# Starts of TensorE's tiles in SBUF: multiples of 128 bytes in the FFNs of a two-layer trunk

## The chip, the cores and the metric

The kernel runs on one core of a Trainium2 chip. The metric is the device time of one execution in microseconds (us), as the median of several runs. TensorE multiplies, VectorE (DVE), ScalarE (ACT) and GpSimd (POOL) do the elementwise work, and SyncE (SP) issues every DMA.

## The reference

A trunk of two layers over 512 positions of 1024 channels, in float32. Each layer is an FFN, a token mixer and a second FFN; layer 0 mixes by causal pooling over windows of 2 to 16 positions, layer 1 by forgetting attention with 16 heads. Each sub-layer first normalises and modulates x by the conditioning vector c:

```python
for i in range(DEPTH):
    mod = (silu(c) @ ada_w[i] + ada_b[i]).reshape(b_, 3, 3, D_MODEL)
    h = adaln(x, norm_g[i, 0], mod[:, 0, 0], mod[:, 0, 1])
    x = x + 0.5 * (1.0 + mod[:, 0, 2]) * swiglu(h, ffn_w_in[i, 0], ffn_w_out[i, 0])
    h = adaln(x, norm_g[i, 1], mod[:, 1, 0], mod[:, 1, 1])
    x = x + (1.0 + mod[:, 1, 2]) * mixer[i](h)
    h = adaln(x, norm_g[i, 2], mod[:, 2, 0], mod[:, 2, 1])
    x = x + 0.5 * (1.0 + mod[:, 2, 2]) * swiglu(h, ffn_w_in[i, 1], ffn_w_out[i, 1])

def swiglu(h, w_in, w_out):          # w_in (1024, 5632), w_out (2816, 1024)
    g, u = jnp.split(h @ w_in, 2, axis=-1)
    return (jax.nn.silu(g) * u) @ w_out
```

## The kernel before

**Layout.** Channels lie on the 128 partitions, positions along them: x is eight tiles of 128 x 512. The four FFNs have the numbers 0, 2, 3 and 5 of the six sub-layers (1 is the pooling, 4 the attention).

**Exact products in three.** A float32 operand is held as two float32r parts, hi and lo: ScalarE copies (and so rounds) the first, VectorE subtracts it from the source for the second (`split`, lines 144 to 150). `mm3` (lines 159 to 162) makes one product out of three matmuls: hi by hi, hi by lo, lo by hi. In the FFNs the held operand (TensorE's weight load, 128 x 128) is a block of the weights, wh or wl, and the streamed one is 512 or 256 columns of the activations: hhi and hlo, the normalised input, in the product "up" (`up`, lines 295 to 305), and gh and gl, the gated values, in the product "down" (lines 344 to 349 and `closing`, line 342).

**Loops.** An FFN goes in three chunks of 8, 8 and 6 of its 22 blocks of hidden channels. Up makes, for each block, two products (gate and value) over 8 tiles of channels: 2 x 8 x 3 = 48 matmuls. `gated` (line 286) makes gh and gl from them. Down takes, for each of the 8 tiles of output channels, the blocks of the chunk: 8 x 8 x 3 = 192 matmuls for a chunk of eight. Most are 512 wide; 256 wide are the first units and the last chunk of the FFNs that stand next to a norm, where the positions are done half by half.

**Weights.** SP loads a unit of weights into `raw` (line 153), in order of need, one DMA a unit; `split` writes wh and wl into the next of the slots (`slot`, line 64). Two slots are in the pool `wts` on the left side; a third, in the pool `more` on the right side, exists in FFNs 0, 2 and 3. The attention uses the same `weights` for its projections; there the held operand is a block of hhi or hlo and the streamed one 256 columns of the weights.

**Order.** SP's queue is in the order of the code in the FFNs; the first stage (before line 767) has SP, VectorE and ScalarE in order too. The other engines' order comes from the framework's list scheduling.

**Where the tiles begin.** The allocator places a tile on a multiple of 32 bytes within the partition, one after the other as the pools and sizes have it. For this program the starts, modulo 128 and modulo 512, are:

| tiles | modulo 128 | modulo 512 |
|---|---|---|
| hhi, hlo (streamed in up) | 32 | 416 |
| gh, gl (streamed in down) | 32 | 288 |
| wh, wl, raw in `wts` | 32 | 288 |
| wh, wl in `more` (third slot) | 96 | 480 |
| attention's q and k, groups 0 and 2 | 64 | 320 |
| attention's q and k, groups 1 and 3 | 32 | 288 |

The steps inside these tiles are 512, 1024 or 2048 bytes, so every slice begins at the same remainder of 128.

**Modulation.** `ada_open` (line 102) makes the small tiles of one sub-layer's modulation (`mods`) when the first work on them is due; they lie in the pool `pers` behind hlo.

Of the kernel before, what the change touches and what calls it, by code (L numbers as in the profile page):

```python
# [33 lines left out]
LAG = 3  # L34
SPAN = 16
EARLY = 4
WHOLE = ((0, S),)
# [4 lines left out]
def trunk(  # L42
# [21 lines left out]
    def slot(shape):  # L64
        """Both parts of a unit of weights, in the next of the slots."""
        pool = slots["pools"][slots["at"] % len(slots["pools"])]
        slots["at"] += 1
        return (pool.tile(shape, F32R, tag="wh", name="wh"), pool.tile(shape, F32R, tag="wl", name="wl"))

    dram = ctx.enter_context(tc.tile_pool(name="dram", bufs=1, space=DRAM))  # L70

    # ---- constants, parameters that stay on chip
    cond = right.tile([P, D], F32, name="cond")
    cst = pers.tile([P, 2, P], F32, name="cst")
    ident = cst[:, 0, :]
    ng = pers.tile([P, DEPTH * 3, KT], F32, name="ng")
    ab = pers.tile([P, DEPTH * 3, 3 * KT], F32, name="ab")
    x = pers.tile([P, KT, S], F32, name="x")
    ones = pers.tile([P, P], F32, name="ones")
    dve.memset(ones, 1.0)  # L80
    mhalf = pers.tile([P, GH], F32, name="mhalf")
    gp.memset(mhalf, -0.5)
    # the one table with all that an FFN takes, before anything waits for it
    act.activation(cond[:, 0:1], mhalf[:, 0:1], AF.Silu)

    # ---- modulation: column (dt, scale|shift) and gates of one sub-layer
    mods = {}

# [5 lines left out]
    def ada_work(i, u, raw):  # L94
        for r in range(2):
# [4 lines left out]
            )  # L100

    def ada_open(i):
        mods[i] = {
            "raw": pers.tile([P, 3 * KT], F32, name=f"mraw{i}"),
            "a": pers.tile([P, KT], F32, name=f"ma{i}"),
            "s": pers.tile([P, KT], F32, name=f"ms{i}"),
            "g": pers.tile([P, KT], F32, name=f"mg{i}"),
        }

# [18 lines left out]
    def ada_jobs(i, with_affine=True):  # L128
        """Pairs of a load and the work on it, for the steps of an FFN."""

        def work(u, raw):
            if u == 0:
                ada_open(i)
            ada_work(i, u, raw)
            if u == KT - 1:
                ada_affine(i, 0, KT)
            if u == KT + 3:
                ada_gate(i, i % 3 != 1)

        return [(lambda pool, u=u: ada_load(i, u, pool), lambda raw, u=u: work(u, raw))  # L140
                for u in range(0 if with_affine else KT, KT + 4)]

    # ---- exact splits of float32 into two float32r parts
    def split(parts, src, pieces=1):
# [7 lines left out]
    def weights(src, shape, pieces=4):  # L152
        raw = wts.tile(shape, F32, tag="raw", name="raw")
        nc.sync.dma_start(raw, src)
        parts = slot(shape)
        split(parts, raw, pieces)
        return parts
# [5 lines left out]

    # ---- pre-norm with adaLN
    hhi = pers.tile([P, KT, S], F32R, name="hhi")
    hlo = pers.tile([P, KT, S], F32R, name="hlo")

# [9 lines left out]
    def sumsq_pe(st, dt, t0, tn):  # L177
        """As sumsq, summed over the partitions too."""
        sq = tmp.tile([P, tn], F32, tag="sq", name="sq")
        act.activation(sq, x[:, dt, t0:t0 + tn], AF.Square)  # L180
        pe.matmul(st[:, :tn], ones, sq, start=dt == 0, stop=dt == KT - 1)  # L181

    def rsig(acc, t0, tn, summed=False):
        """1 / rms of each position, on every partition."""
        b0, bn = t0 // P, tn // P
        v = tmp.tile([P, NTB], F32, tag="v", name="v")
        if summed:
            st = acc
            for b in range(bn):
                bs = slice(b * P, (b + 1) * P)  # L190
                dve.tensor_tensor_reduce(out=st[:, bs], in0=st[:, bs], in1=ident, scale=1.0, scalar=0.0,
                                         op0=ALU.mult, op1=ALU.add, accum_out=v[:, b:b + 1])
            st = v
        else:
            st = bank("s")
            for b in range(bn):
                pe.matmul(st[:, b:b + 1], acc[:, (b0 + b) * P:(b0 + b + 1) * P], ones[:, 0:1],
                          start=True, stop=True)
        dve.tensor_scalar(out=v[:, :bn], in0=st[:, :bn], scalar1=1.0 / D, scalar2=EPS,
                          op0=ALU.mult, op1=ALU.add)  # L200
        gp.tensor_tensor(out=v[:, :bn], in0=v[:, :bn], in1=mhalf[:, :bn], op=ALU.pow)
        dg = tmp.tile([P, bn, P], F32, tag="dg", name="dg", bufs=1)
        dve.tensor_tensor(
            out=dg, in0=ident.unsqueeze(1).to_broadcast([P, bn, P]),
            in1=v[:, :bn].unsqueeze(2).to_broadcast([P, bn, P]), op=ALU.mult)
        r = bank("s")
        pe.matmul(r[:, :bn * P], ones, dg.rearrange("p b t -> p (b t)"), start=True, stop=True)
        return r
# [25 lines left out]

    # ---- half-step SwiGLU
    class Feed:
        """The weights of an FFN, unit by unit, in the order that the products take them."""

# [19 lines left out]
    def ffn(i, feed, jobs, then, begin=None, ahead_by=2, started=None):  # L258
# [3 lines left out]
        def job(pool, behind):  # L262
            """The work of the last load, behind what its engine does in this step; the next load."""
            if loaded:
                work, raw = loaded.pop()
                with tc.issue_after(behind):
                    work(raw)
                if ahead_by == 1:
                    return
            if jobs:  # L270
                load, work = jobs.pop(0)
                loaded.append((work, load(pool)))

        acc = new_acc() if then else None
        with (
# [6 lines left out]
            def g_tile():  # L282
                return (fp.tile([P, S], F32R, tag="gh", name="gh", bufs=JC + 1),
                        fp.tile([P, S], F32R, tag="gl", name="gl", bufs=JC + 1))

# [62 lines left out]
    def closing(wt, n, g, i, acc, then):  # L348
        """The last n tiles of a contraction: x is complete half by half of the positions."""
        for t0, tn in HALVES if then else WHOLE:  # L350
# [10 lines left out]

    # ---- multi-scale causal pooling
    class Pooling:
# [10 lines left out]
        def means(self, r, t0, tn):  # L374
            """Window means less the position itself."""
            m = mods[self.i]
# [39 lines left out]
        def mix(self, made, t0, tn):  # L416
            """The product by group, into x; returns the sums of squares."""
            sums = bank()
# [7 lines left out]

    # ---- forgetting attention
    def fox_first(pool):
        """Weights of the first q and k, ahead of time, in buffers that later hold v, q and k."""
        first = {}  # L430
# [18 lines left out]
    def fox(i, early_pool, first, second_half, then):  # L449
        acc2 = new_acc()  # L450
        with tc.tile_pool(name="fox", bufs=1, reuse_waits="tile") as fp:
            gains = fp.tile([P, 2], F32, name="gains")
            nc.sync.dma_start(gains, fox_gain)
            # the scores are held negated: their minimum is the bias of the exponential
            dve.tensor_scalar(out=gains[:, 0:1], in0=gains[:, 0:1], scalar1=-(HD ** -0.5),
# [5 lines left out]
            def forget():  # L461
                """cumsum(log_sigmoid(f)) by head, to DRAM to be spread over partitions."""
                bf = fp.tile([HEADS, 1], F32, name="bf")
# [17 lines left out]
                dve.scalar_tensor_tensor(out=e, in0=z, scalar=-1.0, in1=z, op0=ALU.mult, op1=ALU.min)  # L481
                # log1p(e) = log(w) + (e - (w - 1)) with w = 1 + e as rounded
                act.activation(e, e, AF.Exp)
# [12 lines left out]
            def projections(grp):  # L496
                """Steps that leave q, k by channel and v by position, split, for one group of heads."""
                made = {}
# [67 lines left out]
            class Head:  # L566
                """One head: scores and softmax by block of queries, then the product with v."""

# [88 lines left out]
            def early(ots):  # L657
                """The output projection of the first EARLY pairs of heads, into x."""
                held = {}
# [32 lines left out]

    # ---- the trunk
    ada_open(0)
    with tc.tile_pool(name="more", bufs=1, side="right", reuse_waits="tile") as more:
# [3 lines left out]
        with tc.tile_pool(name="start", bufs=2, reuse_waits="tile") as sp, in_order, ExitStack() as early:  # L699
            adas0 = early.enter_context(tc.tile_pool(name="adas", bufs=5, reuse_waits="tile"))  # L700
            w4 = early.enter_context(tc.tile_pool(name="w4", bufs=1, reuse_waits="tile"))
            # x by rows: 1 / rms is a scalar of each partition; then the channels to the partitions
            rows = sp.tile([P, NTB, D], F32, name="rows", bufs=1)
# [19 lines left out]
            def some_weights(kt, first=0, last=4):  # L723
                """The columns kt and kt + 1 of the units first .. last."""
                sl = slice(kt, kt + 2)
                if first == 0:
                    pieces[kt] = wts.tile([P, 4, 2, 2, P], F32, tag="raw", name="raw")
                for j in range(first, last):
# [166 lines left out]
```

## Time and profile before

| | us |
|---|---|
| median of 3 runs | 1861.64 |
| lowest and highest | 1855.61, 1865.67 |
| span of the profiled execution, first to last instruction | 1863.7 |
| TensorE busy in it | 1830.7 |
| VectorE, ScalarE, GpSimd busy in it | 985.8, 622.8, 107.0 |

The profile shows one execution; its own time stands in it as the span alone. A matmul's row has its start and a modelled end; since matmuls overlap, the time that one takes is read from its start to the next one's start. "x12" is a count of instructions, "<-" in a tile's name stands between what is written and what is read, and "<-" behind an idle time names what ended it.

### The profile page before, as it was taken

The numbers are of one execution on the slowest core, as the hardware profiler recorded it, in microseconds if no ns is written. First come the engines' busy times: TensorE is split into PE (matmuls) and PEld (weight loads), VectorE is DVE, ScalarE is ACT, GpSimd is POOL, SyncE is SP. The second block draws the span as 40 slices with busy tenths as digits, with TensorE's granted clock in tenths as the row PEclk, the third lists the DMA queues.
The fourth block names the chain that finished last, engine by engine and source line by source line (L and its number), as shares of the span: only waits on it lengthen the run. The fifth ranks groups of instructions, "written<-read, shape, count | busy, mean of one in ns | idle before, by whom it ended". The sixth has DMA issues, their size and how long they took to land.

```text
span 1863.7 us, 23985 instructions
## 1 busy us (share of the span) xinstructions
PE 1830.7 (98%) x9564; PEld 1549.0 (83%) x9564; DVE 985.8 (53%) x1947; ACT 622.8 (33%) x1242; POOL 107.0 (6%) x118
## 2 busy tenths in 40 slices
PE   6999999989999999999999999999999999999999
PEld 5888888879888888998888889988997888888887
DVE  7467466386466473363544534666666553432433
ACT  6323223244213232342222333354444442222221
POOL 0000000040000000110000001321010200000000
PEclk9999999989999999999999999999999899999999
DMA  9456465211266452231543531012111021321421
GB/s 365 181 203 262 178 228 225 92 68 70 112 257 240 169 212 93 73 136 70 199 173 120 190 126 69 25 69 86 63 63 63 30 107 57 124 96 63 135 91 68
DMA packets 45712, 244.66 MB, mean 131 GB/s; under 512 B 5392, under 2 KB 9872, under 8 KB 21792
## 3 DMA queue, kind: packets, MB, share of 16 engines
q1 hardware_dynamic: 45600, 243.13, 35.5%
q8 instruction: 75, 1.23, 0.3%
q14 instruction: 37, 0.30, 0.1%
HBM read 240.98 MB, written 2.13 MB: 130 GB/s over the span
## 4 chain that ended last, share of the span: by engine, by line
PE 96%; DVE 2%; ACT 1%; DMA 0%; issue 0%; SPq 0%; ACTq 0%; DVEq 0%
PE mm L160 29%; PE mm L161 28%; PE mm L162 28%; PE s L160 3%; PE s L161 3%; PE s L162 3%; PE mm L600 1%; PE mm L583 1%; PE mm L422 1%; DVE wl L149 1%; DMA cond<-c_in 0%; DVE x L225 0%; PE mm L181 0%; PE s L543 0%; DVE win L396 0%; DVE ada L97 0%
## 5 line engine op out<-in xcount | busy, mean ns | idle before, releaser
L161 PE MATMUL mm<-hlo,wh 128*128 128x512 f32 (+1 forms) x1512 | 566.8, 376 | 2.6 <-DVE hlo L764 2.6
L162 PE MATMUL mm<-hhi,wl 128*128 128x512 f32 (+1 forms) x1512 | 565.1, 376 | 0.5 <-DVE wl L149 0.5
L160 PE MATMUL mm<-hhi,wh 128*128 128x512 f32 (+1 forms) x1512 | 562.4, 377 | 1.7 <-ACT hhi L755 1.4
L148 ACT ACTIVATE wh<-raw 128x256 fp32r<-128x256 f32 (+2 forms) x528 | 311.4, 654 | 573.5 <-PE mm L161 325.6
L149 DVE TENSOR_TENSOR wl<-raw,wh 128x256 fp32r<-128x256 f32 (+2 forms) x528 | 359.8, 733 | 49.5 <-ACT wh L148 46.0
L161 PEld LDWEIGHTS mm<-hlo,wh 128*128 128x128 f32 x1512 | 283.9, 188 | 59.5 <-DVE hlo L764 3.1
L160 PEld LDWEIGHTS mm<-hhi,wh 128*128 128x128 f32 x1512 | 283.2, 188 | 59.3 <-ACT hhi L755 1.8
L162 PEld LDWEIGHTS mm<-hhi,wl 128*128 128x128 f32 x1512 | 284.0, 188 | 57.2 <-DVE wl L149 0.7
L290 DVE TENSOR_TENSOR sil<-sil,mm 128x512 f32<-128x512 f32 (+1 forms) x95 | 61.0, 642 | 487.0 <-PE mm L162 478.6
L161 PE MATMUL mm<-gl,wh 128*128 128x512 f32 (+1 forms) x848 | 299.1, 353 | 0.0
L162 PE MATMUL mm<-gh,wl 128*128 128x512 f32 (+1 forms) x848 | 298.0, 353 | 0.0
L160 PE MATMUL mm<-gh,wh 128*128 128x512 f32 (+1 forms) x848 | 297.7, 354 | 0.0
L162 PEld LDWEIGHTS mm<-gh,wl 128*128 128x128 f32 x848 | 159.9, 189 | 22.3
L161 PEld LDWEIGHTS mm<-gl,wh 128*128 128x128 f32 x848 | 160.0, 189 | 22.3
L160 PEld LDWEIGHTS mm<-gh,wh 128*128 128x128 f32 x848 | 159.3, 189 | 22.8
L97 DVE CUSTOM_DVE_ANT_0 ada<-ada,cond 128x1024 f32<-128x1024 f32 x144 | 170.1, 1218 | 1.0 <-DMA ada<-ada_w 1.0
L289 ACT ACTIVATE sil<-mm 128x512 f32<-128x512 f32 (+1 forms) x94 | 52.8, 562 | 256.5 <-PE mm L162 255.3
L337 DVE SCALAR_TENSOR_TENSOR x<-mm,mg,x 128x512 f32<-128x512 f32 x64 | 47.9, 749 | 105.3 <-PE mm L162 104.9
L175 POOL TENSOR_TENSOR acc<-acc,sq 128x256 f32<-128x256 f32 x56 | 49.6, 886 | 875.5 <-ACT sq L174 538.7
L160 PE MATMUL s<-wh,hhi 128*128 128x256 f32 x288 | 84.9, 295 | 1.9 <-DVE qk L549 1.9
L162 PE MATMUL s<-wh,hlo 128*128 128x256 f32 x288 | 82.6, 287 | 0.0
L161 PE MATMUL s<-wl,hhi 128*128 128x256 f32 x288 | 82.1, 285 | 0.0
(177 smaller groups left out, 1710.3 us busy)
## 6 DMA issues: line engine op xcount, KB each, us to landing
raw<-w_in SPq DMA_DIRECT2D x84, 1024.0 KB, 4.9
ada<-ada_w SPq DMA_DIRECT2D x72, 1024.0 KB, 4.9
raw<-w_out SPq DMA_DIRECT2D x64, 512.0 KB, 5.6
raw<-w_end SPq DMA_DIRECT2D x12, 1024.0 KB, 4.8
raw<-fox_qkv SPq DMA_DIRECT2D x12, 1024.0 KB, 4.8
raw<-w_in SPq DMA_DIRECT2D x16, 256.0 KB, 8.3
cb<-cum SPq DMA_DIRECT2D x16, 256.0 KB, 3.3
raw<-fox_o SPq DMA_DIRECT2D x4, 1024.0 KB, 4.9
```

The costliest lines, as they stand in the source:

```text
L97: dve.tensor_tensor_reduce(out=raw[:, r, :], in0=raw[:, r, :], in1=cond, scale=1.0, scalar=0.0, op0=ALU.mult, op1=ALU.add, accum_out=mods[ ...
L148: act.activation(hi[:, c:c + n], src[:, c:c + n], AF.Copy)
L149: dve.tensor_tensor(out=lo[:, c:c + n], in0=src[:, c:c + n], in1=hi[:, c:c + n].bitcast(F32), op=ALU.subtract)
L160: pe.matmul(o, lh, rh, start=start, stop=False)
L161: pe.matmul(o, lh, rl, start=False, stop=False)
L162: pe.matmul(o, ll, rh, start=False, stop=stop)
L175: gp.tensor_tensor(out=acc[:, sl], in0=acc[:, sl], in1=sq, op=ALU.add)
L289: act.activation(sil[:, :tn], gu[0][:, :tn], AF.Silu)
L290: dve.tensor_tensor(out=sil[:, :tn], in0=sil[:, :tn], in1=gu[1][:, :tn], op=ALU.mult)
L337: done = dve.scalar_tensor_tensor(out=x[:, dt, :], in0=y, scalar=mods[i]["g"][:, dt:dt + 1], in1=x[:, dt, :], op0=ALU.mult, op1=ALU.add)
L422: pe.matmul(y[:, :tn], self.w[:, 2 * dt + ct], made[dt // 2][:, ct], start=ct == 0, stop=ct == 1)
L583: pe.matmul(s[:, b * P:n], mr[:, 0, :], mr[:, 1, :], start=False, stop=True)
```

## The change

Tiles of the pool `wts` (raw, wh, wl), hhi and hlo, and the FFNs' gh and gl are asked for on multiples of 128 bytes. The weights of the third slot (`more`) and the attention's own tiles are not. The modulation tiles are all made at the head, ahead of x, and `ada_open` with its two calls goes. Comments go too, so that line numbers shift.

```diff
+LINE = 128
...
     def slot(shape):
         pool = slots["pools"][slots["at"] % len(slots["pools"])]
         slots["at"] += 1
-        return (pool.tile(shape, F32R, tag="wh", name="wh"), pool.tile(shape, F32R, tag="wl", name="wl"))
+        line = LINE if pool is wts else None
+        return (pool.tile(shape, F32R, tag="wh", name="wh", align_bytes=line),
+                pool.tile(shape, F32R, tag="wl", name="wl", align_bytes=line))
...
+    mods = {i: {t: pers.tile([P, n], F32, name=f"m{t}{i}")
+                for t, n in (("raw", 3 * KT), ("a", KT), ("s", KT), ("g", KT))}
+            for i in range(DEPTH * 3)}
     x = pers.tile([P, KT, S], F32, name="x")
...
-    mods = {}
...
-    def ada_open(i):
-        mods[i] = {
-            "raw": pers.tile([P, 3 * KT], F32, name=f"mraw{i}"),
-            "a": pers.tile([P, KT], F32, name=f"ma{i}"),
-            "s": pers.tile([P, KT], F32, name=f"ms{i}"),
-            "g": pers.tile([P, KT], F32, name=f"mg{i}"),
-        }
...
-            if u == 0:
-                ada_open(i)
...
     def weights(src, shape, pieces=4):
-        raw = wts.tile(shape, F32, tag="raw", name="raw")
+        raw = wts.tile(shape, F32, tag="raw", name="raw", align_bytes=LINE)
...
-    hhi = pers.tile([P, KT, S], F32R, name="hhi")
-    hlo = pers.tile([P, KT, S], F32R, name="hlo")
+    hhi = pers.tile([P, KT, S], F32R, name="hhi", align_bytes=LINE)
+    hlo = pers.tile([P, KT, S], F32R, name="hlo", align_bytes=LINE)
...
             def g_tile():
-                return (fp.tile([P, S], F32R, tag="gh", name="gh", bufs=JC + 1),
-                        fp.tile([P, S], F32R, tag="gl", name="gl", bufs=JC + 1))
+                return (fp.tile([P, S], F32R, tag="gh", name="gh", bufs=JC + 1, align_bytes=LINE),
+                        fp.tile([P, S], F32R, tag="gl", name="gl", bufs=JC + 1, align_bytes=LINE))
...
-    ada_open(0)
...
                 if first == 0:
-                    pieces[kt] = wts.tile([P, 4, 2, 2, P], F32, tag="raw", name="raw")
+                    pieces[kt] = wts.tile([P, 4, 2, 2, P], F32, tag="raw", name="raw", align_bytes=LINE)
```

## Rows read from the trace of the kernel before

**Rows 1.** The page: span, busy time, share and instructions of each engine.

```profile
span 1863.7 us, 23985 instructions
...
PE 1830.7 (98%) x9564; PEld 1549.0 (83%) x9564; DVE 985.8 (53%) x1947; ACT 622.8 (33%) x1242; POOL 107.0 (6%) x118
```

**Rows 2.** The page: the chain that ended last, by engine.

```profile
PE 96%; DVE 2%; ACT 1%; DMA 0%; issue 0%; SPq 0%; ACTq 0%; DVEq 0%
```

**Rows 3.** Stretches of 50 us: busy us and instructions by engine, granted clock, DMA.

```profile
core 0: us, PE busy (x) PEld busy (x) DVE busy (x) ACT busy (x) POOL busy (x), PEclk, DMA share, GB/s
0.00:50.00 50.00, 33.62 (x141) 26.52 (x142) 36.77 (x83) 31.96 (x52) 1.32 (x6) 1.00 0.94 351
...
250.00:300.00 50.00, 50.00 (x220) 41.12 (x220) 39.83 (x74) 13.34 (x28) 1.08 (x2) 1.00 0.79 300
...
1650.00:1700.00 50.00, 50.00 (x216) 40.24 (x215) 17.78 (x20) 14.40 (x20) 0.00 (x0) 1.00 0.23 82
```

**Rows 4.** Groups of instructions by line and shape: count, busy us, mean ns.

```profile
L161 PE MATMUL mm<-hlo,wh 128*128 128x512 f32 x1256 | 496.1, 395 | 2.6 <-DVE hlo L764 2.6
...
L160 PEld LDWEIGHTS mm<-hhi,wh 128*128 128x128 f32 x1512 | 283.2, 188 | 59.3 <-ACT hhi L755 1.8 <-ACT hhi L218 0.4 <-ACT wh L148 0.3
L161 PE MATMUL mm<-gl,wh 128*128 128x512 f32 x560 | 218.4, 390 | 0.0
...
L161 PE MATMUL s<-wl,hhi 128*128 128x256 f32 x288 | 82.1, 285 | 0.0
L161 PE MATMUL mm<-gl,wh 128*128 128x256 f32 x288 | 80.7, 282 | 0.0
...
L161 PE MATMUL mm<-hlo,wh 128*128 128x256 f32 x256 | 70.6, 283 | 0.0
```

**Rows 5.** Timeline, TensorE, last FFN: ends of 384 up, then 192 down matmuls.

```profile
1626.87 0.40 PE L160 MATMUL mm<-hhi,wh 128*128 128x512 f32 x1
...
1716.46 0.39 PE L160 MATMUL mm<-gh,wh 128*128 128x512 f32 x1
...
1760.00 0.40 PE L160 MATMUL mm<-hhi,wh 128*128 128x512 f32 x1
```

**Rows 6.** Timeline, 256 wide: ends of 84 down, 48 up, 47 down matmuls.

```profile
774.80 0.28 PE L160 MATMUL mm<-gh,wh 128*128 128x256 f32 x1
...
784.88 0.28 PE L160 MATMUL mm<-gh,wh 128*128 128x256 f32 x1
...
821.98 0.28 PE L160 MATMUL mm<-hhi,wh 128*128 128x256 f32 x1
...
827.43 0.28 PE L160 MATMUL mm<-hhi,wh 128*128 128x256 f32 x1
...
1144.49 0.28 PE L160 MATMUL mm<-gh,wh 128*128 128x256 f32 x1
...
1149.82 0.28 PE L162 MATMUL mm<-gh,wl 128*128 128x256 f32 x1
```

**Rows 7.** Timeline, pooling's mix: 16 float32 passes, and what follows them.

```profile
423.92 3.62 PE L422 MATMUL mm<-made,poolw 128*128 128x256 f32 x16
427.38 0.59 PE L181 MATMUL mm<-sq,ones 128*128 128x256 f32 x2
```

**Rows 8.** Timeline, attention's scores: second and third matmul, group 1, then group 2.

```profile
1302.78 0.39 PE L161 MATMUL mm<-qk 64*128 64x512 f32 x1
1303.02 0.39 PE L162 MATMUL mm<-qk 64*128 64x512 f32 x1
...
1355.45 0.39 PE L161 MATMUL mm<-qk 64*128 64x512 f32 x1
1355.68 0.39 PE L162 MATMUL mm<-qk 64*128 64x512 f32 x1
```

## The prediction

> **What bounds the kernel.** I read the page first, its busy times and its chain. TensorE is busy 98% of the span [rows 1], and the chain that ended last is 96% TensorE [rows 2]. So the question is how far apart TensorE's matmuls start. The table by stretches says where that holds: only the first 50 us wait for loads (TensorE busy 33.6 of 50, DMA share 0.94); inside an FFN TensorE is busy without a gap, at a granted clock of 1.00 (2.4 GHz), with 216 to 220 matmuls in 50 us [rows 3]. The groups by shape give the counts. Each line of `mm3` has the same, so I multiply by three: 512 columns wide there are 3 x 1256 matmuls that stream hhi or hlo ("up") and 3 x 560 that stream gh or gl ("down"); 256 wide 3 x 256 up, 3 x 288 down, and 3 x 288 that hold a block of hhi or hlo and stream weights of the attention [rows 4]. That is 3768, 1680 and 2496.
>
> A matmul's duration in the profile (390 to 396 ns) overlaps the next one, so it is no price. The price is the time from start to start, and the timeline gives it. In the last FFN, 384 up matmuls start between 1626.87 and 1716.46: 89.59 / 384 = 233.3 ns each. The 192 down matmuls after them take 43.54 / 192 = 226.8 ns [rows 5]. 512 columns at 2.4 GHz are 213.3 ns. So 20.0 ns of each up matmul and 13.4 ns of each down matmul are not columns, though TensorE never waits for another engine there: together 3768 x 20.0 + 1680 x 13.4 = 98 us of the span. The change can only reach these 98 us and their like in the 256-wide matmuls.
>
> **What the spacings are made of.** Sixteen columns are 64 bytes of a partition and 6.667 ns. In that unit the up matmul takes 35.0 pieces and the down one 34.0, where 512 columns fill 32. The 256-wide ones fill 16: 48 up matmuls with weights from the third slot take 5.45 / 48 = 113.5 ns (17.0 pieces), 84 down ones with weights from `wts` take 10.08 / 84 = 120.0 ns (18.0), 47 down ones with the third slot's weights 5.33 / 47 = 113.4 ns (17.0) [rows 6]. The averages sit on whole pieces, and the excess is one to three of them. A tile that begins 32 bytes past a multiple of 64 spreads its 512 columns over 33 pieces of 64 bytes, and 256 columns over 17. One piece of the excess is what the position of the start would explain.
>
> **The change part by part.** It adds no instruction to any engine and no transfer, and removes none: the modulation tiles (`mods`) are only asked for earlier, `ada_open` issued nothing, and the loops stand as they were. So there is no new wait and nothing is queued anew on SP or elsewhere. By the sizes, gh and gl move up by 96 bytes, which fits. What changes is the start of every operand that the FFNs give to TensorE: hhi, hlo, gh, gl, and the weights in `wts`. The weights in the third slot stay 96 past a multiple of 128.
>
> - *hhi, hlo, gh, gl (streamed).* The trace has no float32r matmul that streams a tile on a multiple of 128, so I bound the price. The best case comes from a float32 product: its 16 passes of 256 columns, at two cycles a column, start in 427.38 - 423.92 = 3.46 us, 216 ns each, against 213.3 ns of columns [rows 7]. At that spacing up gains 17.1 ns and down 10.6 ns. The other end is no gain, or a loss: the worst average that a row shows is 35 pieces, so down could rise from 34 to 35, and up by as much. I take one piece off for each matmul, 6.667 ns, since that is the part which the start explains; it is nearer to the lower end of the gain than to the upper.
>  Up: 3768 x 6.667 ns = 25.1 us. Down: 1680 x 6.667 ns = 11.2 us.
> - *256 wide.* The same piece: (768 + 864 + 864) x 6.667 ns = 16.6 us. The last 864 are the attention's projections, which stream weights from `wts` and so move as well.
> - *Weights in `wts` (held).* A weight load takes 188 ns [rows 4] and runs beside the matmul before it. For 512 columns it is covered by 227 to 233 ns of streaming, so I cost its own change at nothing; without that cover it would cost what the 256-wide rows differ by, 120.0 - 113.4 = 6.6 ns. `raw` is not read by TensorE; its splits on ScalarE and VectorE have room, since TensorE does not wait inside an FFN [rows 3].
> - *First 50 us.* Its 192 up matmuls wait for loads; their 1.3 us gain nothing.
>
> Sum: 25.1 + 11.2 + 16.6 - 1.3 = 51.6 us, against the span of 1863.7 us: 1812. The profiled span is 2.1 us above the median of the runs shown, so I forecast 1810 us. What a faster TensorE triggers: loads come 3% closer together; the busiest FFN stretch has a DMA share of 0.79 [rows 3], which becomes 0.81, so TensorE stays the bound.
>
> **A rule against it.** The Trainium skill's page "SBUF — State Buffer", section "Specifications (TRN2)", gives lines of 16 bytes and a penalty when accesses cross to a new one. All old starts are multiples of 32, thus of 16; by that rule alone no operand crosses one line less, and the sum would be 0 us instead of 51.6: that is the first rival below. The spacings above, which are not a column's time, are not explained by it either.
>
> **Rivals.**
> - *Nothing changes* (the start is not what costs). For it: the attention's scores are a test in the trace. Groups 0 and 2 hold q and k on 64 past a multiple of 128, groups 1 and 3 on 32 past one. From the second to the third of a block's 512-wide score matmuls it is 1355.68 - 1355.45 = 0.23 us for a group on 64, and 1303.02 - 1302.78 = 0.24 us for a group on 32 [rows 8]. That is the same within the rounding, although the first begin on a multiple of 64. Against it: these hold 64 rows, come singly, and neither lies on a multiple of 128. Time: 1862.
> - *All the excess goes* (the port gives whole speed to a start on a multiple of 128). Up 17.1, down 10.6, and 256-wide from 113.4 to 120 towards 109, some 8 ns: 64.4 + 17.8 + 20.0 = 102 us, so 1760 at the best, and 1785 where the third slot's weights, a third of the units in three of the four FFNs, keep part of it. For it: two thirds of the excess is not explained by one piece, and 16 passes at 216 ns show that TensorE can run next to its column time. Against it: these passes read at half the pace. On the Trainium skill's page "TensorE: Matmul & The Clock Gate", section "Wait — 56ns, not 53.3ns?", 512 columns start every 215.7 ns; the FFNs' 233.3 and 226.8 ns disagree with that, and by it the sum would be near this rival's.
> - *Slower: the weight load and the stream meet worse.* Up and down both begin 32 past a multiple of 128 and still differ by 6.5 ns; what differs is how far the streamed tile lies from the held one, modulo 512: 128 bytes for up, 0 for down. After the change up lies 256 away and down 0 (worked out from the sizes). If a start on 128 brings both streams to one place at once, down goes to 35 pieces or up to 36: 1680 x 6.667 = 11 us or 3768 x 6.667 = 25 us, so 1873 to 1898. It decides from 1.7 ns a matmul on (9.3 us over 5448). Against it: 17 pieces for 256 columns exist with a load in every matmul [rows 6], so a load need not cost anything.
>
> **How the numbers follow.** 0.5% is 9.3 us, about what a measurement of this kernel tells from no change. One piece off, wholly or for up alone: 0.41, its own range 1787 to 1837 (from 25 us, up alone, to 75 us, up freed of two pieces and the rest of one). All the excess: 0.18. Nothing: 0.24. Slower: 0.17. Of the first, 0.01 may end within 0.5%. That gives faster 0.58, same 0.25, slower 0.17. For 8 in 10 the range takes in the first three cases and leaves out the slower one and the last of the best one: 1764 to 1871.
>
> **What would show it.** Right: in the last FFN the up matmuls start 226.7 ns apart and the down ones 220.0; the 256-wide ones 107 to 113; the attention's scores unchanged; busy times of ScalarE and VectorE unchanged. Nothing changed: 233.3 and 226.8 again. All: 216 in both. Slower: 233 or more in down, 240 in up. Wrong in kind: TensorE waiting in an FFN, or a stretch there with fewer columns per us though the matmuls are closer. The number is most likely to be wrong in the size of a piece's share: that one of three pieces goes rests on arithmetic alone, and the scores speak against it.

## The result and the profile after

The change makes the kernel slower: 1872.49 us as the median of 6 runs (1868.02 to 1874.45) against 1862.09 us for the kernel before, in 6 runs with it (1855.61 to 1865.67). The ratio is 1.0052, with a 95% interval of 1.0037 to 1.0066: half a per cent, just past the 9.3 us that the prediction set as the bound of "no change". The forecast was 1810 us with a range of 1764 to 1871; the time lies above both.

The page of the changed kernel answers to [rows 1, 2]: span, busy times, and the chain that ended last.

```profile
span 1872.7 us, 23984 instructions
...
PE 1841.4 (98%) x9564; PEld 1550.5 (83%) x9564; DVE 986.0 (53%) x1947; ACT 622.1 (33%) x1242; POOL 106.3 (6%) x118
...
PE 97%; DVE 2%; ACT 1%; DMA 0%; issue 0%; SPq 0%; ACTq 0%
```

The span is 9.0 us longer and TensorE is busy 10.7 us longer. The other engines' busy times are unchanged, and so is the number of matmuls. The chain is still TensorE's. TensorE's instructions stand in the same order in both kernels, so each matmul of after can be set against its twin of before. The stretches that answer to [rows 3], again with busy us and instructions by engine, granted clock and DMA:

```profile
core 0: us, PE busy (x) PEld busy (x) DVE busy (x) ACT busy (x) POOL busy (x), PEclk, DMA share, GB/s
0.00:50.00 50.00, 35.34 (x140) 27.88 (x141) 36.75 (x83) 31.75 (x52) 1.31 (x6) 1.00 0.91 351
250.00:300.00 50.00, 50.00 (x218) 40.45 (x217) 40.50 (x76) 13.13 (x30) 0.41 (x2) 1.00 0.74 283
1650.00:1700.00 50.00, 50.00 (x216) 40.22 (x216) 14.59 (x16) 13.11 (x17) 0.00 (x0) 1.00 0.27 95
```

Inside an FFN TensorE still has no gap, at the same clock (1.00, the level of 2.4 GHz). There are 218 matmuls between 250 and 300 us where there were 220. So nothing new is waited for; the matmuls themselves stand further apart. The timeline of the last FFN shows which, answering to [rows 5]: again the starts at both ends of 384 up matmuls and of the 192 down ones behind them (`mm3` is lines 154 to 156 here).

```profile
1634.41 0.39 PE L154 MATMUL mm<-hhi,wh 128*128 128x512 f32 x1
...
1724.01 0.40 PE L154 MATMUL mm<-gh,wh 128*128 128x512 f32 x1
...
1768.39 0.39 PE L154 MATMUL mm<-hhi,wh 128*128 128x512 f32 x1
```

Up takes (1724.01 - 1634.41) / 384 = 233.3 ns, as before. Down takes (1768.39 - 1724.01) / 192 = 231.1 ns, 4.3 more than the 226.8 of before. The 256-wide stretches that answer to [rows 6], ends of 84 down, 48 up and 47 down matmuls:

```profile
779.65 0.28 PE L154 MATMUL mm<-gh,wh 128*128 128x256 f32 x1
...
789.54 0.28 PE L154 MATMUL mm<-gh,wh 128*128 128x256 f32 x1
...
826.76 0.28 PE L154 MATMUL mm<-hhi,wh 128*128 128x256 f32 x1
...
832.39 0.28 PE L154 MATMUL mm<-hhi,wh 128*128 128x256 f32 x1
...
1151.44 0.28 PE L154 MATMUL mm<-gh,wh 128*128 128x256 f32 x1
...
1157.00 0.28 PE L156 MATMUL mm<-gh,wl 128*128 128x256 f32 x1
```

These go both ways: 9.89 / 84 = 117.7 ns (120.0 before), 5.63 / 48 = 117.3 (113.5), 5.56 / 47 = 118.3 (113.4).

The pairs of score matmuls that answer to [rows 8], whose two operands move alike, take 0.24 and 0.23 us again:

```profile
1310.65 0.40 PE L155 MATMUL mm<-qk 64*128 64x512 f32 x1
1310.89 0.39 PE L156 MATMUL mm<-qk 64*128 64x512 f32 x1
...
1363.38 0.39 PE L155 MATMUL mm<-qk 64*128 64x512 f32 x1
1363.61 0.39 PE L156 MATMUL mm<-qk 64*128 64x512 f32 x1
```

Summed over all matmuls of both traces, from each start to the next one's, the 9.0 us are these:

| matmuls | number | ns before | ns after | difference, us | forecast, us |
|---|---|---|---|---|---|
| up 512, weights from `wts` | 2736 | 232.8 | 233.3 | +1.3 | |
| up 512, third slot | 912 | 233.2 | 234.1 | +0.8 | |
| up 512 together | 3648 | | | +2.2 | -25.1 (+1.3 of the first stage) |
| first stage: 192 up matmuls and the 32 transposes of x among them | 224 | | | +0.1 | 0 |
| down 512, weights from `wts` | 1295 | 227.0 | 231.2 | +5.5 | |
| down 512, third slot | 384 | 229.2 | 232.9 | +1.4 | |
| down 512 together | | | | +6.9 | -11.2 |
| 256 wide in the FFNs | 1632 | | | +0.3 | |
| attention's matmuls with weights | 1152 | | | +0.5 | -16.6 with the row above |
| all other matmuls | 1228 | | | -1.0 | 0 |

(Up's 3648 and the first stage's 192 are the 3768 of [rows 4] and 72 of the first stage that write to other tiles, named `s`; the very last matmul, a down one, has no next start.) The first stage stands by itself because it waits for loads: there the up matmuls take 2.0 us more and the transposes among them 1.9 us less, which says only which of them stood behind a wait. The loss sits in down, with 2.2 us in up (summed before rounding); what was to gain did not.

### The profile page after: what moved, and what is told of

Read it like the earlier page. It is cut to its first block, busy times and chain, and to the rows that moved or that the text cites. A ratio compares the mean times of both kernels' runs of the same rounds, so it can differ in the third digit from the quotient of the medians.

```text
span 1872.7 us, 23984 instructions
## 1 busy us (share of the span) xinstructions
PE 1841.4 (98%) x9564; PEld 1550.5 (83%) x9564; DVE 986.0 (53%) x1947; ACT 622.1 (33%) x1242; POOL 106.3 (6%) x118
## 4 chain that ended last, share of the span: by engine, by line
PE 97%; DVE 2%; ACT 1%; DMA 0%; issue 0%; SPq 0%; ACTq 0%
PE mm L154 29%; PE mm L155 28%; PE mm L156 28%; PE s L154 3%; PE s L156 3%; PE s L155 3%; PE mm L594 1%; PE mm L577 1%; PE mm L416 1%; DVE wl L143 1%; DMA cond<-c_in 0%; PE mm L175 0%; DVE x L219 0%; PE s L537 0%; DVE win L390 0%; PE s L201 0%
```

## The experiments

Two theories were set against each other. **S**: what costs is where a tile starts. **D**: what costs is how far the streamed tile lies from the held one. The starts in the changed kernel, as its allocation has them, modulo 512: hhi and hlo 128; wh 0 and wl 128; gh 256 and gl 384; the third slot 480 as before. Asking for a multiple of 128 leaves 128 bytes between the two tiles of a pair, so wl no longer begins at the same remainder of 256 as wh, nor gl as gh. Before, each pair did. The third theory of the first expectation, C, is spelt out there.

**m512: 512 columns, all places.** A kernel of matmuls alone: 48 of them for each of 16 x 16 places of the streamed and of the held tile, 32 bytes apart, 512 columns of float32r, one held block of 128 columns each.

```python
COMBOS = [(m, h) for h in range(0, 512, 32) for m in range(0, 512, 32)]
    for m0, h0 in COMBOS:
        for k in range(EACH):
            m = m0 // 4 + S * (k % KT)
            h = h0 // 4 + P * (k % (2 * KT))
            nc.tensor.matmul(acc[:, :N], held[:, h:h + P], moving[:, m:m + N],
                             start=n == 0, stop=n == total - 1)
```

> A kernel of matmuls alone, 512 columns wide in float32r: 256 pairs of starts (streamed tile at 0 to 480 bytes past a multiple of 2048, held tile at 0 to 480 past one, in steps of 32), 48 matmuls for each pair; its output is no trunk. Theory D (distance: what counts is how far the streamed tile lies from the held one modulo 512): the spacing is the same along each diagonal of the table, about 226.7 ns at distance 0, 231.2 at 256, 233.3 at 128, whatever the start modulo 128. Theory S (start: what counts is where the streamed tile itself begins): the spacing is the same along each column, 233 for 0 and 227 to 233 for 32, whatever the held tile's place. Theory C (neither: what differs is up and down, their order of hi and lo parts): one spacing all over the table.

Four rows of its timeline, each 40 like matmuls run together: the start of the first, the time to the end of the last, so 39 spacings and one duration of about 0.39. The streamed and held tiles begin at 128 and 0, at 32 and 32, at 0 and 128, and at 256 and 256.

```profile
61.98 9.49 PE L42 MATMUL mm<-moving,held 128*128 128x512 f32 x40
...
207.07 9.23 PE L42 MATMUL mm<-moving,held 128*128 128x512 f32 x40
...
730.71 9.49 PE L42 MATMUL mm<-moving,held 128*128 128x512 f32 x40
...
1532.77 9.23 PE L42 MATMUL mm<-moving,held 128*128 128x512 f32 x40
```

(9.49 - 0.39) / 39 = 233.3 ns and (9.23 - 0.39) / 39 = 226.7 ns. A tile 32 past a multiple of 128 runs as fast as one on a multiple of 256, when the other operand begins at the same remainder. The whole table of 256 places has one pattern:

| streamed less held, modulo 256 | 0 | 32 | 64 | 96 | 128 | 160 | 192 | 224 |
|---|---|---|---|---|---|---|---|---|
| ns from start to start (last 39 spacings of 48) | 226.7 | 233.3 | 228.9 | 233.3 | 233.4 | 234.2 | 233.4 | 233.4 |

It is the same along each diagonal within 0.1 ns, but for four places 128 apart (232.5 to 233.2). S and C fall. D holds, with one amendment: the table repeats after 256 bytes, where the expectation had 512. And it gives the spacings of before: up, 128 apart, 233.4 (233.3 measured); down, 0 apart, 226.7 (226.8); third slot, 192 apart in up and 64 in down, 233.4 and 228.9 (233.2 and 229.2 in the table above).

**m256: the same with 256 columns.** `N = 256`, nothing else.

> The same table for 256 columns; its output is no trunk. Theory D: the spacing goes by distance alone, from 113.3 to 120 ns. Theory S: it goes by the streamed or the held tile's own start: 113.4 where the held tile lies 96 past a multiple of 128, 118 to 120 elsewhere. Theory C: one spacing.

Measured, by the same eight distances: 120.0, 117.8, 117.8, 120.1, 118.6, 118.7 (some 117.3), 117.8 (some 113.3), 118.3 ns, again with a period of 256. Here distance 0 is among the dearest: at 256 columns the tiles are better apart. So 256-wide rows can go either way; the 84 down ones, at distance 0 before, took these 120.0 ns. But distance does not settle it alone. The 47 down ones of before lie 64 from the third slot's weights and took 113.4, where this table has 117.8. And with the streamed tile at 192 and the held one at 0, this kernel and the later m_cols differ. First this kernel at distance 0 (256 and 0), then at 192 and 0, then m_cols at 192 and 0, 40 matmuls each:

```profile
62.34 4.96 PE L42 MATMUL mm<-moving,held 128*128 128x256 f32 x40
...
50.99 4.88 PE L42 MATMUL mm<-moving,held 128*128 128x256 f32 x40
...
227.40 4.70 PE L46 MATMUL mm<-moving,held 128*128 128x256 f32 x40
```

(4.96 - 0.28) / 39 = 120.0, (4.88 - 0.28) / 39 = 117.9 and (4.70 - 0.28) / 39 = 113.3 ns. The last two have the same two starts; what differs is what ran just before them (distance 160 here, 128 there). That something carries over from one matmul to the next is a guess from this; no run was made for it.

**e1_up_distance: only up's distance, the old starts.** The kernel before with a 128-byte tile behind hlo, which moves `wts`, gh and gl by 128; hhi and hlo stay. All of these begin 32 past a multiple of 128, now all at 416 modulo 512; the third slot stays at 480.

```diff
     hlo = pers.tile([P, KT, S], F32R, name="hlo")
+    pad = pers.tile([P, 32], F32, name="pad")
+    gp.memset(pad, 0.0)
```

> The kernel before with a tile of 128 bytes behind hlo: hhi, hlo, wts, gh and gl then all begin at 416 modulo 512 (32 past a multiple of 128, as before), so up's distance goes from 128 to 0 for weights in wts. Theory D: up with wts from 232.8 to 226.7 ns, 2832 x 6.1 = 17 us less: 1845 us; down unchanged at 226.8. Theory S: hhi's and hlo's start modulo 512 is unchanged (416) and down's goes from 288 to 416, so down rises to up's 233: 1680 x 6 = 10 us more, 1872 us. Theory C: 1862.

Measured 1849.2 us (1848.8 to 1851.44) against 1863.4; ratio 0.9929 (0.9912 to 0.9946). The last FFN in its timeline, at the same three places as above:

```profile
1617.34 0.39 PE L160 MATMUL mm<-hhi,wh 128*128 128x512 f32 x1
...
1704.37 0.39 PE L160 MATMUL mm<-gh,wh 128*128 128x512 f32 x1
...
1747.89 0.39 PE L160 MATMUL mm<-hhi,wh 128*128 128x512 f32 x1
```

Up falls to 87.03 / 384 = 226.6 ns with no start on a multiple of 128; down stays at 43.52 / 192 = 226.7. D is right on the effect and 4 us too hopeful on the time. By the tally that was used above, up with weights from `wts` gave 16.2 of its 17 us; what it left out is down with the third slot's weights, now 192 from them, which lost 1.5 us (229.2 to 233.1 ns), and the FFNs' 256-wide matmuls, which lost 2.2.

**e2_down_distance: the changed kernel with gh and gl moved.** 256 bytes ahead of gh.

```diff
+            pad = fp.tile([P, 64], F32, name="pad", bufs=1)
+            gp.memset(pad, 0.0)
```

> The changed kernel with a tile of 256 bytes ahead of gh and gl: all starts stay on multiples of 128, down's distance goes from 256 to 0. Theory D: down with wts from 231.2 to 226.7 ns, some 7 us of the 10 lost come back: 1865 us; up unchanged at 233.3. Theory S: starts modulo 128 are what they were, so the spacings stay: 1872 us. Theory C: 1872.

A miss: 1872.26 us (1867.29 to 1874.61), ratio to before 1.0046 (1.0028 to 1.0064). The last FFN:

```profile
1632.27 0.39 PE L154 MATMUL mm<-hhi,wh 128*128 128x512 f32 x1
...
1721.87 0.40 PE L154 MATMUL mm<-gh,wh 128*128 128x512 f32 x1
...
1766.25 0.39 PE L154 MATMUL mm<-hhi,wh 128*128 128x512 f32 x1
```

Up stays at 89.60 / 384 = 233.3 ns and down at 44.38 / 192 = 231.1. With a period of 256 the move is none at all, and S and C, which had 1872, fall only by m512. What was left to separate 231.1 from 226.7 in down was the two parts of a pair, which no longer begin alike; m3 tries that.

**m3: triples.** Matmuls in the order of `mm3` (wh with gh, wh with gl, wl with gh), for 8 x 8 x 8 places: d is gh less wh, a is gl less gh, b is wl less wh.

```python
    for d, a, b in COMBOS:
        for k in range(TRIPLES):
            for w, g in (("wh", "gh"), ("wh", "gl"), ("wl", "gh")):
                m = (d if g == "gh" else d + a) // 4 + S * k
                h = (0 if w == "wh" else b) // 4 + P * k
                nc.tensor.matmul(acc, tiles[w][:, h:h + P], tiles[g][:, m:m + S],
                                 start=n == 0, stop=n == total - 1)
```

> A kernel of matmuls alone in the FFNs' pattern (wh by gh, wh by gl, wl by gh; 512 columns), for 8 x 8 x 8 places of the tiles modulo 256: d is gh's distance from wh, a gl's from gh, b wl's from wh, 24 matmuls for each; its output is no trunk. Theory D-own (the distance of the two operands of one matmul counts): the mean of three cells of the table of m512, for d, d + a and d - b; at d = 0, a = b = 128 that is (226.7 + 233.4 + 233.4) / 3 = 231.2 ns. Theory D-next (the distance to the held tile that is loaded for the next matmul counts): cells for d, d + a - b and d, at the same place 226.7 ns. Both: 226.7 at d = a = b = 0, and the changed kernel's up (d = 128, a = 0, b = 128) 231.2 where it measured 233.3; if the table gives 233.3 there, single cells can't be added.

In its timeline, the ends of 15 spacings at (0, 128, 128), the changed kernel's down, and at (128, 0, 128), its up:

```profile
222.42 0.39 PE L40 MATMUL mm<-gh,wh 128*128 128x512 f32 x1
...
225.88 0.40 PE L40 MATMUL mm<-gh,wh 128*128 128x512 f32 x1
...
1469.50 0.39 PE L40 MATMUL mm<-gh,wh 128*128 128x512 f32 x1
...
1473.00 0.39 PE L40 MATMUL mm<-gh,wh 128*128 128x512 f32 x1
```

3.46 / 15 = 230.7 and 3.50 / 15 = 233.3 ns: the changed kernel's 231.1 and 233.3, within the rounding of two rows (0.7 ns over 15 spacings). So the pair's own offset is enough to make the loss. D-next falls, which had 226.7 for the first. D-own, the mean of the three matmuls' prices in m512, gives (226.7 + 233.4 + 233.4) / 3 = 231.2 for both; that is near for the first and 2 ns off for the second. Of the 512 places nearly all lie between 228.3 and 236 ns, none at 226.7 but that where all four tiles begin alike (its own block stands at the cold start of this kernel; e1 has it). Prices of single matmuls can't be added where distances are mixed.

**e3_all_distances: the third slot too.** e1, and 64 bytes on the right side that bring the third slot to the same remainder.

```diff
+    shift = right.tile([P, 16], F32, name="shift")
+    gp.memset(shift, 0.0)
```

> As e1, and 64 bytes more on the right side, so that the third slot's weights begin at 416 modulo 512 too: every distance in the FFNs is 0. Theory D: the third slot's up and down matmuls, 233.4 ns in e1, come to 226.7 as well: (966 + 384) x 6.7 = 9 us less than e1, 256-wide ones some 1 us more: 1841 us. Theory S: starts modulo 128 go from 96 to 32 for these weights: as e1, 1849 us.

Measured 1840.94 us (1837.49 to 1843.13) against 1862.24; ratio 0.9885 (0.9867 to 0.9902). That beats both kernels, the changed one by 31.6 us. In the timeline, the ends of 48 up matmuls with weights from the third slot, and the last FFN:

```profile
835.37 0.39 PE L162 MATMUL mm<-hhi,wh 128*128 128x512 f32 x1
...
846.25 0.39 PE L162 MATMUL mm<-hhi,wh 128*128 128x512 f32 x1
...
1609.04 0.39 PE L162 MATMUL mm<-hhi,wh 128*128 128x512 f32 x1
...
1696.08 0.39 PE L162 MATMUL mm<-gh,wh 128*128 128x512 f32 x1
...
1739.60 0.39 PE L162 MATMUL mm<-hhi,wh 128*128 128x512 f32 x1
```

10.88 / 48 = 226.7 ns with the third slot, and 226.7 in the last FFN, up and down. By the tally that was used above, up 512 gains 16.6 us with weights from `wts` and 6.0 with the third slot, down 512 1.5, and the FFNs' 256-wide matmuls lose 4.7, as m256 says of distance 0.

**e4_both: the starts on multiples of 512, and alike.** The kernel before with 96 bytes ahead of hhi and 128 behind hlo, so that hhi, hlo, gh, gl and `wts` all begin on multiples of 512. The third slot stays as it was.

```diff
+    pads = [pers.tile([P, 24], F32, name="pad0")]
     hhi = pers.tile([P, KT, S], F32R, name="hhi")
     hlo = pers.tile([P, KT, S], F32R, name="hlo")
+    pads.append(pers.tile([P, 32], F32, name="pad1"))
+    for pad in pads:
+        gp.memset(pad, 0.0)
```

> The kernel before with 96 bytes ahead of hhi and 128 behind hlo: hhi, hlo, gh, gl and the weights in wts then all begin on multiples of 512, so the change's aim (multiples of 128) is met, and all their distances are 0. Theory D: as e1, 1849 us, up and down with wts 226.7 ns, with the third slot (distance 32) 233.3. Theory S, starts on 128 cost: as the changed kernel, 1872 us, down at 231. Theory S, starts on 128 gain beside the distances: below e1 by 6.7 ns a matmul, 1820 us or less.

Measured 1851.74 us (1848.38 to 1853.6); ratio 0.9943 (0.9928 to 0.9957). The last FFN:

```profile
1619.02 0.39 PE L160 MATMUL mm<-hhi,wh 128*128 128x512 f32 x1
...
1706.06 0.39 PE L160 MATMUL mm<-gh,wh 128*128 128x512 f32 x1
...
1749.58 0.39 PE L160 MATMUL mm<-hhi,wh 128*128 128x512 f32 x1
```

226.7 and 226.7 ns, as in e1: in these matmuls the start on a multiple of 512 is worth nothing, and costs nothing. By the tally, what e4 takes more than e1 lies outside the FFNs (1.2 us in the attention's matmuls with weights, 2.1 in all other matmuls). What e1 and e4 share, and the changed kernel lacks, is that all operands begin alike.

**e5_no_line: the changed kernel's distances on the old starts.** The kernel before with 128 bytes between wh and wl, 128 ahead of gh and 128 between gh and gl. No start is on a multiple of 128.

```diff
+        wh = pool.tile(shape, F32R, tag="wh", name="wh")
+        if pool is wts and "pad" not in slots:
+            slots["pad"] = wts.tile([P, 16], F32, tag="pad", name="pad")
...
+                if first:
+                    pad("pad1")
+                gh = fp.tile([P, S], F32R, tag="gh", name="gh", bufs=JC + 1)
+                if first:
+                    pad("pad2")
```

> The kernel before with 128 bytes between wh and wl, 128 ahead of gh and 128 between gh and gl: all starts stay 32 past a multiple of 128, but the distances modulo 256 are those of the changed kernel (wh and gh alike, wl and gl 128 further, hhi and hlo 128 from wh). Theory D: the changed kernel's spacings without its alignment: down 231.2, up 233.3 ns, 1872 us. Theory S: the spacings of before: down 226.8, up 232.8 ns, 1862 us.

Measured 1869.34 us (1867.27 to 1871.66); ratio 1.0039 (1.0024 to 1.0055). The last FFN:

```profile
1629.72 0.39 PE L164 MATMUL mm<-hhi,wh 128*128 128x512 f32 x1
...
1719.32 0.40 PE L164 MATMUL mm<-gh,wh 128*128 128x512 f32 x1
...
1763.70 0.39 PE L164 MATMUL mm<-hhi,wh 128*128 128x512 f32 x1
```

233.3 and 44.38 / 192 = 231.1 ns: the loss of the changed kernel, without the starts that the change is about. S, with 1862, falls. The time is 3 us under the changed kernel's 1872, the profiled execution 4.7 us. By the tally, 1.7 us of that lie with the third slot, whose distance differs by 32 (230.7 instead of 232.9 ns in down, 233.3 instead of 234.1 in up), and 2.2 in the row of all other matmuls, which no run followed up.

**m_width: does the load's length make the excess?** m512 at eight distances, with held blocks of 128, 96, 64 and 32 columns.

> A kernel of matmuls alone, 512 columns streamed, with held tiles of 128, 96, 64 and 32 columns at 8 distances (0 to 224), 48 matmuls for each; its output is no trunk. It asks what the 13.4 ns are that stay at distance 0. Theory B (beside: the load of the next held tile meets the stream, each meeting costing a part of a piece, so a shorter load meets it less often): the excess over 213.3 ns shrinks with the held columns, towards 216 ns at 32 columns, and so do the differences between distances. Theory F (fixed: a float32r stream runs 17/16 slower by itself): 226.7 ns at distance 0 for every width, and only the differences between distances shrink.

The groups of weight loads by shape (count, busy us, mean ns), then two rows of 39 matmuls at distance 0, held 128 and 32 columns wide:

```profile
L41 PEld LDWEIGHTS mm<-moving,held 128*128 128x128 f32 x1152 | 217.9, 189 | 66.0 <-ACT held L32 14.4
...
L41 PEld LDWEIGHTS mm<-moving,held 128*32 128x32 f32 x384 | 41.6, 108 | 47.3
```

```profile
107.73 9.00 PE L41 MATMUL mm<-moving,held 128*128 128x512 f32 x39
...
374.21 9.20 PE L41 MATMUL mm<-moving,held 128*32 128x512 f32 x39
```

The load shrinks from 189 to 108 ns, but the spacing at distance 0 grows, from (9.00 - 0.39) / 38 = 226.6 to (9.20 - 0.40) / 38 = 231.6 ns. Over the eight distances the means stay between 228.4 and 233.4 ns at every width under 128. The difference between the dearest and the cheapest distance shrinks as both theories had it, from 7.5 ns at 128 held columns to 5.0, 4.4 and 2.8 at 96, 64 and 32. The rest of both falls: the excess neither goes with the load nor stays at 226.7.

**m_cols: a share of the columns, or once in a matmul?** Distances 0, 64, 128 and 192, with 512 down to 256 streamed columns, then 512 columns of bfloat16.

> A kernel of matmuls alone, full held tiles, 48 for each case: 512, 448, 384, 320 and 256 columns streamed in float32r at distances 0, 64, 128 and 192, then 512 columns in bfloat16 at the same four; its output is no trunk. It asks what the excess over a column's time belongs to. Theory R (rate: a float32r stream takes 17 cycles for 16 columns): at distance 0 the excess grows with the columns, 13.4 ns at 512, 10 at 384, 8 at 320; bfloat16, half the bytes, stands near 216 ns at every distance. Theory M (each matmul pays once, whatever its length): the excess at distance 0 is 13 ns at every number of columns, and bfloat16 pays it too.

| columns | 0 | 64 | 128 | 192 | columns alone | excess at 0 |
|---|---|---|---|---|---|---|
| 512 | 226.7 | 228.9 | 232.5 | 233.3 | 213.3 | 13.4 |
| 448 | 202.7 | 200.0 | 203.9 | 202.2 | 186.7 | 16.0 |
| 384 | 173.3 | 173.3 | 176.1 | 174.6 | 160.0 | 13.3 |
| 320 | 146.7 | 146.7 | 146.7 | 146.7 | 133.3 | 13.4 |
| 256 | 120.0 | 117.8 | 118.7 | 113.3 | 106.7 | 13.3 |
| 512, bfloat16 | 215.8 | 215.8 | 215.8 | 215.8 | 213.3 | 2.5 |

The rows of 512 columns, float32r at distance 0 and bfloat16 at distance 128, 39 matmuls each, and the group of bfloat16's loads:

```profile
66.50 9.00 PE L46 MATMUL mm<-moving,held 128*128 128x512 f32 x39
...
298.65 8.58 PE L53 MATMUL mm<-moving,held 128*128 128x512 bf16 x39
```

```profile
L53 PEld LDWEIGHTS <-held 128*128 128x128 bf16 x192 | 18.7, 98 | 22.7 <-issue 0.3
```

(9.00 - 0.39) / 38 = 226.6 ns and (8.58 - 0.38) / 38 = 215.8 ns. For float32r the excess at distance 0 is 13.3 ns at every width but 448 (16.0): it is paid once in a matmul, not per column, which is theory M; R, a share of the columns, falls on that. It is no floor, since 256 columns at distance 192 have 113.3 - 106.7 = 6.6. At 512 columns and distance 128 this kernel has 232.5 where m512 has 233.4 at the same starts, a second sign that what ran before counts. In bfloat16 it is 2.5 ns and the distance counts for nothing: there R was right, and M wrong. The Trainium skill's page "TensorE: Matmul & The Clock Gate", section "Wait — 56ns, not 53.3ns?", has 215.7 ns for 512 columns; the bfloat16 rows agree with it, and no float32r row does.

## Why the prediction was wrong

- **The step that failed** is "I take one piece off for each matmul, 6.667 ns, since that is the part which the start explains". The start explains no part: in the last FFN all starts on multiples of 512 give what all starts at 416 give (e4 against e1, 226.7 ns in both), and the changed kernel's loss comes without its starts (e5). The excess that differs between up and down is set by the distance of the streamed from the held tile modulo 256, and by all parts agreeing in it. The arithmetic on pieces of 64 bytes fitted because the means at these distances happen to sit near multiples of 6.667 ns; m512 has 228.9 and 234.2 as well, which don't.
- **Its three terms.** Up: 25.1 us were to go; 2.2 were added outside the first stage. It was 128 bytes from its weights before and stays so for two of its three matmuls. Down: 11.2 were to go; 6.9 were added: from one distance of 0 for all to 0, 128 and 128. The 256-wide: 16.6 were to go; 0.8 were added, the sum of both signs.
- **The rival that came true** is the slower one, in kind: it read off the trace that up and down begin alike and differ only in the distance to the weights. It had 0.17. That its lower end, 1873, is the measured time is luck: it had 11 us from down alone, at 35 pieces; down went to 231.1 / 6.667 = 34.7 pieces and gave 6.9 us of the 9.0, and its own sign, 233 or more in down and 240 in up, was not met. Three things in it were off. It feared that operands come to one place at once, and at 512 columns one place for both is the cheapest (226.7 ns in m512). It took the distance modulo 512, where the period is 256. And it worked out the changed kernel's starts from the sizes, as if wh and wl, and gh and gl, still began alike; the two tiles of a pair have lain 128 bytes apart modulo 256 since the request. Of the four tiles of a triple, it looked at one pair of them.
- **The row that spoke against the step was right.** The scores on 64 and on 32 took the same time before [rows 8], and the prediction said so and took 0.24 from it. Its sum rested on arithmetic alone, as its last part says; the distance to the weights could have been tried on the kernel before: down streams gh and gl from the same starts with either weights, and took 227.0 ns at distance 0 (`wts`) and 229.2 at 64 (third slot).
- **The rival "nothing changes".** It is right on the alignment by itself (e4 and e1 apart by 2.5 us of 1850, no spacing of the last FFN different), as the Trainium skill's page "SBUF — State Buffer", section "Specifications (TRN2)", would have it with its lines of 16 bytes; but no run here shows these lines, and the section says nothing that would give 226.7 against 233.3.
- **What held.** No instruction and no wait was added, loads and VectorE stayed covered, the bound stayed TensorE's spacing, the first stage gained nothing. The 20.0 and 13.4 ns of excess were read rightly. That 13.3 of them stay in a 512-wide float32r matmul at the best place tried (m512, m_cols) limits what a placement gave here: e3, 21.3 us under before, not the 102 us of the best rival.

**What stays open.** What the 13.3 ns are: they go neither with the columns (m_cols) nor with the load's length (m_width), and bfloat16 doesn't pay them. Why mixed distances don't add up (m3), why a narrower block is dearer at distance 0, and whether what ran before is what parts m256 from m_cols. Why the distance counts at all is open too: m_width speaks against a price that goes with the load's length, and no run had matmuls without loads. And the row of all other matmuls: against before it moved between 0.2 us more (e4) and 3.6 us less (e3), with 1.0 less in the changed kernel; no run looked for it.

## What to carry to other kernels

Where TensorE is the bound, read the spacing of its matmuls from start to start, and set it against the columns' own time; if two like groups differ, list the start of every operand, streamed and held, and look at their differences before their alignment. A request for alignment moves what comes behind it and opens gaps between tiles that lay together: read the new addresses of all operands, not only of those that it names. For 512-wide float32r products of this kind, let all operands begin at the same remainder of 256 bytes (here 1.2% for two small pads), and let 256-wide ones not.

## What the runs showed of the hardware that was not expected

- A float32r matmul of 512 columns starts 226.7 to 234.2 ns after the one before it by the distance of its operands modulo 256 bytes, at a granted clock of 1.00 and with a load of 189 ns beside every one (m512, m_width). Of the 256 places of m512, 252 agree with their distance's spacing within 0.1 ns, and the other four within 0.9.
- At 256 columns the order turns: 120.0 ns at distance 0, 117.8 at 64, and 113.3 or 117.8 at 192, both of them for the same two starts in two kernels (m_cols, m256). At 320 columns the distance doesn't count (146.7 at all four).
- In bfloat16 no distance counts (215.8 ns at all four), and a load takes 98 ns.
- A narrower held block, with a load of 108 instead of 189 ns, makes the 512-wide matmul at distance 0 dearer, not cheaper (231.6 ns against 226.6).
